# Queries and keys of an encoder layer: keys first in eight stages with open sums in PSUM, queries as ordinary products

## The chip, the cores and the metric

One core of a Trainium2 chip runs the whole program once. The metric is the time of the kernel on the device in microseconds, as the median of several runs. Five engines work side by side and wait for each other by semaphores: TensorE (PE in the profile, with its weight loads as PEld) multiplies matrices into PSUM; VectorE (DVE), ScalarE (ACT) and GpSimd (POOL) do the elementwise work; SyncE (SP) issues the loads and stores.

## What is computed

One layer of a streaming encoder for 512 prompt tokens and 32 sample tokens, model width 1024. Only the start matters here: a conditioning vector `c` gives scale and shift (`w_ada`), the normalized input is modulated to `h`, and `h` is multiplied with `w_in`, whose first 512 columns are the queries of the attention and whose next 512 are its keys.

```python
mod = jnp.einsum('bd,de->be', jax.nn.silu(c), w_ada) + b_ada
sh1, sc1, g1, sh2, sc2, g2 = jnp.split(mod[:, None, :], 6, axis=-1)
h = layer_norm(x) * (1 + sc1) + sh1
z = jnp.einsum('btd,de->bte', h, w_in)
a_q, a_k, a_v, m_qk, m_v, m_if, m_o = jnp.split(z, IN_SPLITS, axis=-1)
a_out = attend(aq, ak, av, lam)                  # differential attention, 4 heads
m_out, m_state = recur(mq, mk, mv, ig, lf)       # mLSTM, 4 heads, chunkwise
y_a = a_n.astype(x.dtype) @ w_br_a
y_b = m_n.astype(x.dtype) @ w_br_b
mix = (g_a * y_a + g_b * y_b) @ w_o
x = layer_norm(ALPHA * x + (1 + g1) * mix, ln1_g, ln1_b)
ffn = (jax.nn.silu(gt) * up) @ w_down            # after the same adaLN scheme, h2 @ w_gu
```

The keys themselves are an output too (`k_rows`), as tokens by features.

## The kernel before

All activations stand as features by tokens: `h` is eight tiles of 128 features by 544 tokens, each in two parts, `hH` and `hL` (a rounded value and what the rounding left), and each weight tile is split likewise into `hi` by ScalarE and `lo` = raw - `hi` by VectorE or POOL. A product of one 128-column tile of weights (an n-tile) with one feature tile takes three matmuls (`hi` with `hH`, `hi` with `hL`, `lo` with `hH`) for each half of the tokens, 256 and 288 columns, the halves named in `HALF`.

At the start, `x_tile` normalizes the four tiles of prompt tokens and transposes them to `xT`, `x_rows` does the sample's rows. `ada_gemv` makes scale and shift of some feature tiles: sixteen small matmuls into a bank `ga`, copied to `gs`; its transposes `gt` are reduced into `modT`, and `modulate` makes `hH` and `hL` from `xT`. The string `ORDER0` sets the order of these steps up to the second half of the first stage.

Queries and keys are made in five stages of 1, 1, 2, 2 and 2 feature tiles (`STAGES`). In each stage `group_split` splits the stage's key columns, then its query columns; for each of the eight n-tiles a `Unit` opens a PSUM bank of the tag `g` (three buffers), runs the stage's matmuls and closes it, and `qk_evac` copies the bank to `qk` (stage 0) or adds it to what the earlier stages left there: by VectorE (`SCALAR_TENSOR_TENSOR` at L176, or ScalarE's `qk_t` and a POOL addition in stage 1). In the last stage each key head is transposed to tokens by features and stored (`k_out`: `k_tok`, `kst`, `k2`).

After that come ordinary products over all eight feature tiles, run by `stream`, which prepares the next unit's weights while one runs: values, gates, the mLSTM's inputs, branch products, output projection and feed-forward. The attention and the mLSTM are a side stream of generators that `Lane` places between the matmuls of the main stream by its own estimates of when each engine is free; so the place of every side instruction in an engine's queue follows from those estimates. The last product of the second branch reads the mLSTM's result `mna`, `mnb`, made from the transposes `onT` for each head of the sample by `gate_split`. All engines' queues run in the order in which they are written.

Weights come by `load` on SP's queue. Raw weights have a ring of two 8 KB buffers (`raw_tile`), and the first stages' weights lie in slots that later tensors take.

Of the kernel before, what the change touches and what calls it, by code (L numbers as in the profile page):

```python
# [33 lines left out]
class Lane:  # L34
    """Emits the steps of generators between the steps of a main stream, by estimates of when each engine gets there."""
# [58 lines left out]
def trunk_kernel(ctx: ExitStack, tc: tile.TileContext, I: dict, O: list):  # L94
# [16 lines left out]
    class Halves:  # L111
        """Eight tiles of features by tokens, held in the two halves of a slot."""
# [103 lines left out]
    ADA_AT = (0, 0)  # L216
    WARM = 0
    STAGES = (1, 1, 2, 2, 2)
    START = tuple(sum(STAGES[:i]) for i in range(len(STAGES)))
    ada_raw, w_raw = {}, {}  # L220

    def load_ada(s, dst):
        w = STAGES[s] * 128
        if not isinstance(dst, list):
            dst = [dst[:, 8 * i * w:8 * (i + 1) * w] for i in range(2)]
        ada_raw[s] = [d[:, 0:8 * w].rearrange("p (k c) -> p k c", k=8) for d in dst]
        for i in range(2):
            c0 = 1024 * i + START[s] * 128
            load(ada_raw[s][i], w_ada[:, c0:c0 + w].rearrange("(k p) c -> p k c", p=128))
# [11 lines left out]
    s2a = [slot(f"2{c}", [128, 2176], F32, f"s2_a{c}") for c in "ab"]  # L241
    s3a = [slot(f"3{c}", [128, 2176], F32, f"s3_a{c}") for c in "ab"]
    s8a = slot(8, [128, 2048], F32, "s8_a")
# [10 lines left out]
    load_ada(0, raw_tile())  # L254
    load_w(0, raw_tile())
# [105 lines left out]
    warm = bank("o", "warm")  # L361

    def keep_warm(n):
        for _ in range(n):
            tr(warm[:, 0:128], ident, 128)
# [50 lines left out]
    def modulate(k, part=None):  # L416
        """Features of tile k: all tokens, or those of one half."""
# [9 lines left out]
        (vtt if part != 0 else gtt)(hL(k)[:, c], t[:, c], hH(k)[:, c].bitcast(F32), SUB)  # L427

    def all_of(gen):
        for _ in gen:  # L430
            pass

    def ada_gemv(s):
        n = STAGES[s]
        w = n * 128
        ga = bank("o" if s % 2 else "x", "ga")
        for i in range(2):
            for k in range(8):
                g = 32 * (k % 4)
                nc.tensor.matmul(  # L440
                    ga[g:g + 32, i * w:(i + 1) * w], scT[:, k, :], ada_raw[s][i][:, k, :], start=(k < 4), stop=(k >= 4)
                )
                lane.pe(0.06 * n)
        return ga

    def ada_first(s, ga=None, part=None):
        n = STAGES[s]
        w = n * 128
        if ga is None:
            ga = ada_gemv(s)  # L450
        yield 0
        gs = tmp([128, 512], "gs")
        vcopy(gs[:, 0:2 * w], ga[:, 0:2 * w])
        yield 0
        gt = bank("x", "gt")
        for b in range(2 * n):
            tr(gt[:, b * 128:(b + 1) * 128], gs[:, b * 128:(b + 1) * 128], 128)
        yield 0
        red = small([128, 4, 2], "red")
        nc.vector.tensor_reduce(  # L460
            out=red[:, 0:2 * n, :], axis=AX.X, op=ADD,
            in_=gt[:, 0:2 * w].rearrange("p (e g c) -> p e c g", g=4, c=32)[:, :, 0:2, :],
        )
        m = modT[:, 0:16, :].rearrange("p (i k) r -> p i k r", i=2)[:, :, START[s]:START[s] + n, :]
        b = PT[:, c_b_ada:c_b_ada + 16].rearrange("p (i k) -> p i k", i=2)[:, :, START[s]:START[s] + n]
        for i in range(2):
            vtt(
                m[:, i], red[:, i * n:(i + 1) * n, :], b[:, i].unsqueeze(2).to_broadcast([128, n, 2]), ADD
            )
        yield 0  # L470
        ms = [modulate(START[s] + k, part) for k in range(n)]
        for g in ms:
            next(g)
        yield 0
        for g in ms:
            all_of(g)

    groups = [(s, i) for s in range(len(STAGES)) for i in range(2)]
    parts = {}

    def group_split(x):
        if x in parts or x >= len(groups):
            return
        s, i = groups[x]
        n = STAGES[s]
        r = w_raw[s][:, i]
        hi = wp.tile([128, 2, 512], F32R, tag="hi", name="hi", bufs=2)
        lo = wp.tile([128, 2, 512], F32R, tag="lo", name="lo", bufs=2)
        act(hi[:, 0:n], r, AF.Copy)
        gtt(lo[:, 0:n], r, hi[:, 0:n].bitcast(F32), SUB)  # L490
        parts[x] = (hi, lo)
# [4 lines left out]
    def first_half():  # L496
        for x in range(2):
            hi, lo = parts[x]
            for h in range(4):
                ps = bank("g", "g")  # L500
                c = slice(128 * h, 128 * h + 128)
                for p, (w, a) in enumerate(((hi, hH), (hi, hL), (lo, hH))):
                    nc.tensor.matmul(ps[:, 0:256], w[:, 0, c], a(0)[:, 0:256], start=(p == 0), stop=(p == 2))
                act(qk_holder["kq"[x]][:, h, 0:256], ps[:, 0:256], AF.Copy, scale=0.125 if x else 1.0)
                yield
# [3 lines left out]
    g0 = None  # L509
    m1 = None  # L510
    fh = first_half()

    def step(c):
        nonlocal g0, m1, ga1
        if c in "0123":
            next(xg[int(c)], None)
        elif c == "r":
            next(xg[4], None)
        elif c == "c":
            next(pc, None)  # L520
        elif c == "g":
            if g0 is None:
                g0 = ada_first(0, ada_gemv(0), 0)
            next(g0, None)
        elif c == "w":
            group_split(len(parts))
        elif c == "h":
            next(fh, None)
        elif c == "m":
            if m1 is None:  # L530
                m1 = modulate(0, 1)
            next(m1, None)
        elif c == "a":
            ga1 = ada_gemv(1)
        elif c == "p":
            load_params(prm_b)

    ga1 = None
    for c in ORDER0:
        step(c)  # L540
    params(prmB, 64)
    load_w(3, raw_tile())
    load_ada(4, slot(6, [128, 4096], F32, "s6_a"))
    load_w(4, raw_tile())
# [26 lines left out]
    class Unit:  # L571
        """One n-tile of a product: its weights' parts, its matmuls, what takes its results."""
# [38 lines left out]
    class IfUnit:  # L611
        """The gates' eight columns: the weights' two parts side by side, so that each half of h passes once."""
# [112 lines left out]
    def to_tok(src, name, tag="x", part=(0, 1)):  # L725
        """[128, T] features by tokens into PSUM as tokens by features: the prompt's four tiles, the sample's."""
# [108 lines left out]
    def qk_evac(s, i, h):  # L835
        def f(ps, hf, o, n):
            dst = qk_holder["kq"[i]][:, h, o:o + n]
            sc = 0.125 if i else 1.0
            if s == 0:
                act(dst, ps[:, 0:n], AF.Copy, scale=sc)  # L840
            elif s == 1 and hf:
                t = tmp([128, 288], "qk_t")
                act(t, ps[:, 0:n], AF.Copy, scale=sc)
                gtt(dst, dst, t, ADD)
            else:
                stt(dst, ps[:, 0:n], sc, dst, MUL, ADD)
                if hf and s == len(STAGES) - 1:
                    if i:
                        q_tasks.append(lane.add(q_split(h)))
                    else:  # L850
                        lane.add(k_out(h), 0.5)
        return f
# [636 lines left out]
    def stage_part(x, j):  # L1489
        def f():  # L1490
            group_split(x)
            if j == 1:
                group_split(x + 1)
            c = slice(j * 128, (j + 1) * 128)
            return tuple(t[:, :, c] for t in parts[x])
# [615 lines left out]
```

## Time and profile before

| | |
|---|---|
| median of 3 runs | 963.54 us (962.74 to 964.62) |
| span of the profiled execution | 966.0 us |
| mean granted TensorE clock in it | 0.982 |
| first key product, first value product | 18.72 us, 98.70 us |
| TensorE, VectorE, ScalarE, POOL busy | 95%, 54%, 37%, 22% |
| moved by DMA | 110.43 MB, 114 GB/s on average |

The profiled execution is one of its own; of it the span from first to last instruction is known, 2.5 us above the median of the runs. In a row of a timeline stand start and duration of an instruction or a run of like ones, then engine, line of the kernel, operation, what it writes and reads, shapes, and in brackets how long the engine was idle before and who ended that. A row of a list of waits gives who waited for whom, the sum in us, how often, and the longest. In a row of stretches stand busy time and count for each engine, the granted clock of TensorE as a share of full speed, the share of the DMA engines and GB/s. A row of groups gives the count, busy time and mean ns of one, then idle time ahead of them. A matmul's duration overlaps with the next one's, so the distance of two starts is what counts.

### The profile page before, as it was taken

Reading aid. Unit: us, or ns where it says so; the run is one execution under the profiler, and the core shown is the slowest. Engines: PE = TensorE matmul, PEld = TensorE weight load, DVE = VectorE, ACT = ScalarE, POOL = GpSimd, SP = SyncE. Lnnn points to the kernel's source line nnn. Section 1 sums busy time; section 2 is a strip of 40 time slices with the busy share of each in tenths; the row PEclk is TensorE's granted clock in tenths of the full one; section 3 lists DMA queues with packets and bytes.
Section 4 is the critical chain, followed back from the end, with each engine's and each line's share of the span. In section 5 each row is a group of like instructions: output and inputs, shape, how many; then the busy total and the mean of one; then the engine's idle time right before and its main releaser. Section 6 shows DMA issues by size and latency. Waiting matters only on the chain. (4 is left out here: it accounts for less than half of the span.)

```text
span 966.0 us, 17335 instructions
## 1 busy us (share of the span) xinstructions
PE 916.9 (95%) x7184; PEld 868.2 (90%) x7184; DVE 525.4 (54%) x1113; ACT 355.8 (37%) x689; POOL 214.1 (22%) x253
## 2 busy tenths in 40 slices
PE   4799999999999999999999989999999999999993
PEld 4679998798798889899999989999999999999993
DVE  4657567877554444446846886544444443223356
ACT  4511466555542332322434474322222222212241
POOL 4433116332411100101741664200000000000014
PEclk8989999999999999999999999999999999999997
DMA  9904423252244244333911502022222226322302
GB/s 281 337 1 127 147 67 112 88 174 89 88 132 143 93 141 133 93 132 124 309 63 45 192 32 89 1 88 88 89 88 88 88 88 232 123 77 77 121 1 92
DMA packets 92283, 110.43 MB, mean 114 GB/s; under 512 B 3897, under 2 KB 75789, under 8 KB 92205
## 3 DMA queue, kind: packets, MB, share of 16 engines
q1 hardware_dynamic: 91996, 109.27, 34.8%
q8 instruction: 56, 0.92, 0.4%
q14 instruction: 23, 0.18, 0.1%
q10 hardware_dynamic: 208, 0.07, 0.0%
HBM read 102.09 MB, written 7.24 MB: 113 GB/s over the span
## 5 line engine op out<-in xcount | busy, mean ns | idle before, releaser
L153 DVE TENSOR_TENSOR lo<-raw,hi 128x1024 fp32r<-128x1024 f32 (+3 forms) x102 | 112.0, 1098 | 130.4 <-ACT hi L132 125.4
L132 ACT ACTIVATE hi<-raw 128x1024 fp32r<-128x1024 f32 (+2 forms) x124 | 122.1, 984 | 153.1 <-PE dn L600 61.6
L600 PE MATMUL dn<-act,hi 128*128 128x288 f32 (+1 forms) x704 | 135.8, 292 | 0.0
L600 PE MATMUL g<-hHa,hi 128*128 128x288 f32 (+1 forms) x344 | 109.1, 317 | 6.2 <-DVE qka L176 4.7
L600 PEld LDWEIGHTS dn<-act,hi 128*128 128x128 f32 x704 | 110.8, 189 | 0.0
L600 PE MATMUL g<-hHb,hi 128*128 128x256 f32 (+1 forms) x352 | 107.8, 306 | 1.3 <-DVE qka L176 1.3
L600 PE MATMUL g<-h2Ha,lo 128*128 128x288 f32 (+1 forms) x352 | 101.4, 288 | 2.4 <-POOL lo L157 1.5
L600 PE MATMUL dn<-act,lo 128*128 128x288 f32 (+1 forms) x352 | 101.8, 289 | 1.8 <-DVE lo L153 1.8
L600 PE MATMUL g<-h2La,hi 128*128 128x288 f32 (+1 forms) x352 | 101.4, 288 | 1.0 <-DVE h2La L153 1.0
L600 PE MATMUL g<-h2Ha,hi 128*128 128x288 f32 (+1 forms) x352 | 102.1, 290 | 0.0
L600 PE MATMUL g<-hLb,hi 128*128 128x256 f32 (+1 forms) x352 | 101.9, 289 | 0.0
L600 PE MATMUL g<-hLa,hi 128*128 128x288 f32 (+1 forms) x344 | 101.2, 294 | 0.8 <-DVE hLa L153 0.7
L600 PE MATMUL g<-h2Hb,hi 128*128 128x288 f32 (+1 forms) x352 | 101.8, 289 | 0.0
L600 PE MATMUL g<-h2Lb,hi 128*128 128x288 f32 (+1 forms) x352 | 101.5, 288 | 0.1
L600 PE MATMUL g<-hHb,lo 128*128 128x256 f32 (+1 forms) x352 | 101.4, 288 | 0.0
L600 PE MATMUL g<-hHa,lo 128*128 128x288 f32 (+1 forms) x344 | 100.7, 293 | 0.2 <-DVE lo L153 0.2
L600 PE MATMUL g<-h2Hb,lo 128*128 128x288 f32 (+1 forms) x352 | 100.8, 286 | 0.0
L157 POOL TENSOR_TENSOR lo<-raw,hi 128x1024 fp32r<-128x1024 f32 (+2 forms) x30 | 63.6, 2122 | 137.1 <-ACT hi L132 126.5
L600 PEld LDWEIGHTS g<-hHa,hi 128*128 128x128 f32 x344 | 66.0, 192 | 23.0 <-issue 6.2
L280 POOL TENSOR_SCALAR rs__10439<-mv__10423 128x1 f32<-128x1 f32 x1 | 0.2, 190 | 322.4 <-DVE mv__10423 L172 322.4
L600 PEld LDWEIGHTS g<-hHb,hi 128*128 128x128 f32 x352 | 66.7, 190 | 5.3 <-issue 2.7
L600 PEld LDWEIGHTS g<-h2Ha,lo 128*128 128x128 f32 x352 | 66.3, 188 | 3.1 <-POOL lo L157 2.0
(490 smaller groups left out, 2180.4 us busy)
## 6 DMA issues: line engine op xcount, KB each, us to landing
raw<-in_w_gu_dram SPq DMA_DIRECT2D x18, 1024.0 KB, 5.1
raw<-in_w_ada_dram SPq DMA_DIRECT2D x16, 1024.0 KB, 5.2
raw<-in_w_in_dram SPq DMA_DIRECT2D x10, 1024.0 KB
raw<-in_w_gate_dram SPq DMA_DIRECT2D x8, 1024.0 KB, 6.7
raw<-in_w_down_dram SPq DMA_DIRECT2D x8, 1024.0 KB, 5.3
wo<-in_w_o_dram SPq DMA_DIRECT2D x4, 1024.0 KB
rawg<-in_w_gu_dram SPq DMA_DIRECT2D x4, 1024.0 KB
raw<-in_w_down_dram SPq DMA_DIRECT2D x3, 768.0 KB
```

The costliest lines, as they stand in the source:

```text
L132: nc.scalar.activation(out=out, in_=in_, func=func, **kw)
L153: nc.vector.tensor_tensor(out=out, in0=in0, in1=in1, op=op)
L157: nc.gpsimd.tensor_tensor(out=out, in0=in0, in1=in1, op=op)
L280: nc.gpsimd.tensor_scalar(out=out, in0=in_, scalar1=scale, scalar2=EPS, op0=MUL, op1=ADD)
L600: nc.tensor.matmul(ps[:, 0:n], w[:, self.k0 + k, :], a(self.ak0 + k)[:, o:o + n], start=(self.first and k == 0 and p == 0), stop=(self.las ...
```

## The change

Keys alone are made in the first part, in eight equal stages of one feature tile. Their sums stay open in PSUM over all stages: six banks (three of `g`, two of `s`, one of `o`), the first halves of two heads sharing one bank. `qk_evac` is gone; the keys are copied once, after the last stage. The modulation (`ada_gemv`, `ada_turn`, `modulate`) runs two stages ahead of the products. The queries follow in four ordinary units over all eight feature tiles, two loads of 1 MB. Weights' `lo` and the first half's `hL` are made by VectorE in this part instead of POOL.

```diff
-    STAGES = (1, 1, 2, 2, 2)
-    ORDER0 = "0p0c1c1wwg0gg21grgr2ghrhhh3hr2r3hr3hrammh"
...
     def load_w(s, dst):
-        n = STAGES[s]
-        w_raw[s] = dst[:, 0:1024 * n].rearrange("p (i k c) -> p i k c", i=2, k=n)
-        for i, c0 in enumerate((512, 0)):
-            r0 = START[s] * 128
-            load(w_raw[s][:, i], w_in[r0:r0 + n * 128, c0:c0 + 512].rearrange("(k p) c -> p k c", p=128))
+        w_raw.append(dst)
+        load(dst, w_in[s * 128:(s + 1) * 128, 512:1024])
...
-    load_ada(1, s8a)
-    load_w(1, s7a[:, 3072:4096])
-    load_ada(2, s2a)
-    load_w(2, s7a[:, 1024:3072])
-    load_ada(3, s3a)
+    for s in range(1, KD):
+        load_stage(s)
...
-        (vtt if part != 0 else gtt)(hL(k)[:, c], t[:, c], hH(k)[:, c].bitcast(F32), SUB)
+        vtt(hL(k)[:, c], t[:, c], hH(k)[:, c].bitcast(F32), SUB)
...
+    def k_split(s):
+        hi = wp.tile([128, 512], F32R, tag="hi", name="hi", bufs=2)
+        lo = wp.tile([128, 512], F32R, tag="lo", name="lo", bufs=2)
+        act(hi, w_raw[s], AF.Copy)
+        vtt(lo, w_raw[s], hi.bitcast(F32), SUB)
+        k_parts0[s] = hi, lo
...
+    def acc_open(hf):
+        if hf == 0:
+            for i in range(2):
+                b = bank("g", "k_acc")
+                for j in range(2):
+                    acc[2 * i + j, 0] = b[:, 256 * j:256 * j + 256]
+        else:
+            for h, tag in enumerate("gsso"):
+                acc[h, 1] = bank(tag, "k_acc")[:, 0:288]
...
+    def k_mm(s, h, hf, passes):
+        hi, lo = k_parts0[s]
+        o, n = HALF[hf]
+        c = slice(128 * h, 128 * h + 128)
+        for p in passes:
+            w, a = ((hi, hH), (lo, hH), (hi, hL))[p]
+            nc.tensor.matmul(
+                acc[h, hf], w[:, c], a(s)[:, o:o + n],
+                start=(s == 0 and p == 0 and (hf == 1 or h % 2 == 0)),
+                stop=(s == KD - 1 and p == 2 and (hf == 1 or h % 2 == 1)),
+            )
...
+    acc_open(0)
+    gs = ada_gemv(1)
+    k_mms(0, (0,), (0, 1, 2))
+    next(xg[3])
...
+    for s in range(1, KD):
+        ahead = s + 2 < KD
+        if ahead:
+            gs = ada_gemv(s + 2)
+        k_mms(s, (0,), (0, 1, 2))
+        if ahead:
+            ada_turn(s + 2, gs)
+            mods[s + 2] = modulate(s + 2)
+            next(mods[s + 2])
+        if s == KD - 1:
+            for h in range(NH):
+                act(qk_holder["k"][:, h, 0:256], acc[h, 0], AF.Copy)
+        k_mms(s, (1,), (0, 1, 2))
+        if ahead:
+            next(mods[s + 2], None)
+            k_split(s + 2)
+    for h in range(NH):
+        act(qk_holder["k"][:, h, 256:T], acc[h, 1], AF.Copy)
...
+    for h in range(NH):
+        lane.add(k_out(h), 1.0 + 2.0 * h)
+    for c in range(2):
+        units += hunits(w_in, c * 256, [q_evac(2 * c), q_evac(2 * c + 1)])
     units.append(Call(lambda: lane.add(setup())))
```

`q_evac` copies a bank to the queries' tensor with the factor 0.125 and, after the second half, starts `q_split`.

On TensorE's queue at the start, from the sample's first statistics product `cmb` on, stands before:

```order
L136 MATMUL cmb<-mv__248,quart 128x2
L503 MATMUL g<-hHa,hi 128x256
L503 MATMUL g<-hLa,hi 128x256
L503 MATMUL g<-hHa,lo 128x256
L503 MATMUL g<-hHa,hi 128x256
```

and now:

```order
L136 MATMUL cmb<-mv__256,quart 128x2
L418 MATMUL ga<-raw,scT 32x128 x16
L471 MATMUL k_acc<-hHa,hi 128x256
L471 MATMUL k_acc<-hHa,lo 128x256
L471 MATMUL k_acc<-hLa,hi 128x256
L471 MATMUL k_acc<-hHa,hi 128x256
```

The second stage's `ga` has moved ahead of the first key product, and the third pass of a product is now the one with `hL`.

Where keys end and queries begin there was no such place before, since both ran in each stage; now ScalarE's queue has there (`qkb` is the keys' tensor, `qka` the queries'):

```order
L132 ACTIVATE hi<-s_a 128x512
L132 ACTIVATE qkb<-k_acc 128x256 x4
L132 ACTIVATE qkb<-k_acc 128x288 x4
L132 ACTIVATE head_row<-ident 32x4
L132 ACTIVATE hi<-raw 128x1024 x2
L132 ACTIVATE qka<-g 128x256
```

and VectorE's:

```order
L147 TENSOR_SCALAR mn_144<-PT 128x4
L153 TENSOR_TENSOR lo<-raw,hi 128x1024 x2
L180 COPY kst<-k_tok_812 128x512
L180 COPY k_820<-k_tok_817 32x128
L180 COPY kst<-k_tok_823 128x512
```

So the first query weights' `hi` stands behind all evacuations of the keys, and the first copy to `kst` behind two `lo`. On TensorE the transposes of the first two heads follow each other after the first three query products.

At the end of the first branch (products with `ana`, `anb`; the second branch reads `mna`, `mnb`) TensorE's queue was before:

```order
L600 MATMUL g<-ana,lo 128x288
L142 MATMUL onT<-ident,on 128x32 x4
L600 MATMUL g<-ana,hi 128x288
L600 MATMUL g<-anb,hi 128x288
L600 MATMUL g<-ana,lo 128x288
L600 MATMUL g<-ana,hi 128x256
```

and 23 more products of that branch followed. Now:

```order
L142 MATMUL onT<-ident,on 128x32 x4
L609 MATMUL g<-ana,hi 128x288
L609 MATMUL g<-anb,hi 128x288
L609 MATMUL g<-ana,lo 128x288
L609 MATMUL g<-mna,hi 128x256
L609 MATMUL g<-mnb,hi 128x256
```

The sample's `onT` has moved 24 products later; only three products stand between it and the second branch.

More of the change, by code (lines that the diff above doesn't have):

```diff
@@ L214, in trunk_kernel @@
     w_in = I["w_in"][0]
-    ADA_AT = (0, 0)
-    WARM = 0
-    STAGES = (1, 1, 2, 2, 2)
-    START = tuple(sum(STAGES[:i]) for i in range(len(STAGES)))
-    ada_raw, w_raw = {}, {}
+    ada_raw, w_raw = [], []
     def load_ada(s, dst):
[L223 to L226, printed above, removed]
+        ada_raw.append([dst[:, 1024 * i:1024 * i + 1024].rearrange("p (k c) -> p k c", k=8) for i in range(2)])
         for i in range(2):
-            c0 = 1024 * i + START[s] * 128
-            load(ada_raw[s][i], w_ada[:, c0:c0 + w].rearrange("(k p) c -> p k c", p=128))
+            c0 = 1024 * i + s * 128
+            load(ada_raw[s][i], w_ada[:, c0:c0 + 128].rearrange("(k p) c -> p k c", p=128))
     def load_w(s, dst):
-        n = STAGES[s]
-        w_raw[s] = dst[:, 0:1024 * n].rearrange("p (i k c) -> p i k c", i=2, k=n)
-        for i, c0 in enumerate((512, 0)):
-            r0 = START[s] * 128
-            load(w_raw[s][:, i], w_in[r0:r0 + n * 128, c0:c0 + 512].rearrange("(k p) c -> p k c", p=128))
+        w_raw.append(dst)
+        load(dst, w_in[s * 128:(s + 1) * 128, 512:1024])
     x_t = slot(6, [128, 4, D], F32, "x_t")
@@ L240, in trunk_kernel @@
     x_s = s7a[:, 0:256]
-    s2a = [slot(f"2{c}", [128, 2176], F32, f"s2_a{c}") for c in "ab"]
-    s3a = [slot(f"3{c}", [128, 2176], F32, f"s3_a{c}") for c in "ab"]
-    s8a = slot(8, [128, 2048], F32, "s8_a")
+    w_k = s7a[:, 256:4352].rearrange("p (s c) -> p s c", s=KD)
     def load_rows(dst, src):
@@ L253, in trunk_kernel, with load_stage @@
     load_x(1)
-    load_ada(0, raw_tile())
-    load_w(0, raw_tile())
+    ada_at = [raw_tile(), raw_tile()] + [slot(i, [128, 2048], F32, f"s{i}_a") for i in (8, "2a", "2b", "3a", "3b", "5a")]
+    def load_stage(s):
+        load_ada(s, ada_at[s])
+        load_w(s, w_k[:, s, :])
+    load_stage(0)
     load_x(2)
@@ L359, in trunk_kernel @@
     xT = Halves(4, F32, "xT")
[L361 to L365, printed above, removed]
     def x_tile(tt):
@@ L426, in modulate @@
         yield 0
-        (vtt if part != 0 else gtt)(hL(k)[:, c], t[:, c], hH(k)[:, c].bitcast(F32), SUB)
-    def all_of(gen):
-        for _ in gen:
-            pass
+        vtt(hL(k)[:, c], t[:, c], hH(k)[:, c].bitcast(F32), SUB)
     def ada_gemv(s):
-        n = STAGES[s]
-        w = n * 128
-        ga = bank("o" if s % 2 else "x", "ga")
+        ga = bank("x", "ga")
         for i in range(2):
@@ L440, in ada_gemv @@
                 nc.tensor.matmul(
-                    ga[g:g + 32, i * w:(i + 1) * w], scT[:, k, :], ada_raw[s][i][:, k, :], start=(k < 4), stop=(k >= 4)
+                    ga[g:g + 32, 128 * i:128 * i + 128], scT[:, k, :], ada_raw[s][i][:, k, :], start=(k < 4), stop=(k >= 4)
                 )
[L443 to L454, printed above, removed]
+                lane.pe(0.06)
@@ L455, in ada_first, with ada_turn @@
+        gs = tmp([128, 256], "gs")
+        vcopy(gs, ga[:, 0:256])
+        return gs
+    def ada_turn(s, gs):
         gt = bank("x", "gt")
-        for b in range(2 * n):
+        for b in range(2):
             tr(gt[:, b * 128:(b + 1) * 128], gs[:, b * 128:(b + 1) * 128], 128)
-        yield 0
-        red = small([128, 4, 2], "red")
+        red = small([128, 2, 2], "red0")
         nc.vector.tensor_reduce(
-            out=red[:, 0:2 * n, :], axis=AX.X, op=ADD,
-            in_=gt[:, 0:2 * w].rearrange("p (e g c) -> p e c g", g=4, c=32)[:, :, 0:2, :],
-        )
@@ L464, in ada_first @@
[L464 to L491, printed above, removed]
+            out=red, axis=AX.X, op=ADD,
@@ new lines, in ada_turn @@
+            in_=gt[:, 0:256].rearrange("p (e g c) -> p e c g", g=4, c=32)[:, :, 0:2, :],
+        )
+        m = modT[:, 0:16, :].rearrange("p (i k) r -> p k i r", i=2)[:, s]
+        b = PT[:, c_b_ada:c_b_ada + 16].rearrange("p (i k) -> p k i", i=2)[:, s]
+        vtt(m, red, b.unsqueeze(2).to_broadcast([128, 2, 2]), ADD)
+    k_parts0 = {}
+    def k_split(s):
[4 more added lines that the diff above has]
+        k_parts0[s] = hi, lo
@@ L493, in trunk_kernel @@
     qk_holder = {}
     qk_holder["q"], qk_holder["k"] = Halves(5, F32, "qk").h
[L496 to L505, printed above, removed]
+    acc = {}
@@ L507, in trunk_kernel, with k_mms @@
+    def k_mms(s, halves, passes):
+        for hf in halves:
+            for h in range(NH):
+                k_mm(s, h, hf, passes)
     xg = [x_tile(tt) for tt in range(4)] + [x_rows()]
     pc = silu_c()
[L509 to L536, printed above, removed]
@@ L538, in trunk_kernel @@
-    ga1 = None
-    for c in ORDER0:
-        step(c)
-    params(prmB, 64)
-    load_w(3, raw_tile())
-    load_ada(4, slot(6, [128, 4096], F32, "s6_a"))
-    load_w(4, raw_tile())
+    for c in "0":
+        next(xg[0])
+    load_params(prm_b)
+    next(xg[0])
+    next(pc)
+    next(xg[1])
+    next(pc, None)
+    k_split(0)
+    next(xg[1])
+    gs = ada_gemv(0)
+    next(xg[0], None)
+    ada_turn(0, gs)
+    first = modulate(0, 0)
+    next(xg[2])
+    next(xg[1], None)
+    next(first)
+    next(xg[4])
@@ new lines, in trunk_kernel @@
+    next(first, None)
+    next(xg[2])
+    next(xg[4], None)
+    acc_open(0)
+    gs = ada_gemv(1)
+    k_mms(0, (0,), (0, 1, 2))
+    next(xg[3])
+    next(xg[4], None)
+    next(xg[2], None)
+    ada_turn(1, gs)
+    next(xg[4], None)
+    next(xg[3])
+    next(xg[4], None)
+    next(xg[3], None)
+    for g in xg:
+        for _ in g:
+            pass
+    k_split(1)
+    params(prmB, 64)
+    second = modulate(0, 1)
+    next(second)
+    mods = {1: modulate(1)}
+    next(second, None)
+    acc_open(1)
@@ new lines, in trunk_kernel @@
+    next(mods[1])
+    gs = ada_gemv(2)
+    k_mms(0, (1,), (0, 1, 2))
+    next(mods[1], None)
+    ada_turn(2, gs)
+    mods[2] = modulate(2)
+    next(mods[2])
+    k_split(2)
+    next(mods[2], None)
+    for s in range(1, KD):
[14 more added lines that the diff above has]
+            k_split(s + 2)
@@ L833, in setup, with q_evac @@
             yield 0
-    def qk_evac(s, i, h):
+    def q_evac(h):
         def f(ps, hf, o, n):
[L837 to L851, printed above, removed]
+            act(qk_holder["q"][:, h, o:o + n], ps[:, 0:n], AF.Copy, scale=0.125)
+            if hf:
+                q_tasks.append(lane.add(q_split(h)))
         return f
@@ L1487, in trunk_kernel @@
     SIDE_AT = 3
[L1489 to L1495, printed above, removed]
-        return f
-    fin = {}
-    def start_ada(s):
-        return lambda: fin.update({s: lane.add(ada_first(s))})
     lane.free = dict.fromkeys(lane.free, lane.t)
     lane.chain = lane.t
-    fin[1] = lane.add(ada_first(1, ga1))
-    def need_h(s):
-        return lambda: lane.until(lambda: fin[s][2])
-    for x, (s, i) in enumerate(groups):
-        for h in range(4):
-            u = Unit(
-                None, 0, STAGES[s], hH, hL, qk_evac(s, i, h), ak0=START[s], split=stage_part(x, h),
-                halves=(0, 1) if s else (1,),
-            )
-            if i + h == 0 and s:
-                u.need = need_h(s)
-            units.append(u)
-            if (i, h) == ADA_AT and 0 < s and s + 1 < len(STAGES):
-                units.append(Call(start_ada(s + 1)))
+    for h in range(NH):
+        lane.add(k_out(h), 1.0 + 2.0 * h)
+    for c in range(2):
+        units += hunits(w_in, c * 256, [q_evac(2 * c), q_evac(2 * c + 1)])
     units.append(Call(lambda: lane.add(setup())))
@@ L1533, in trunk_kernel @@
     units += vq
-    vch = [u.chunk for u in units if u.chunk]
-    vch[0].gate = lambda: 7 in parts
-    vch[-1].gate = lambda: 9 in parts
     units.append(IfUnit())
```

1 line of the change is left out of this document (added).

## The prediction

> **What bounds the kernel now.** I read the page first, then the list of waits over the first 95 us, the busy time in short stretches, and the timelines of TensorE, VectorE and ScalarE up to the first value product and around 455 us.
>
> ```profile
> span 966.0 us, 17335 instructions
> PE 916.9 (95%) x7184; PEld 868.2 (90%) x7184; DVE 525.4 (54%) x1113; ACT 355.8 (37%) x689; POOL 214.1 (22%) x253
> ...
> PE g L600 <- DVE qka L176: 6.0, 3, 3.5
> ...
> PE g L600 <- ACT qka L132: 1.5, 1, 1.5
> ```
>
> TensorE is busy 95% of the span. Whatever moves the end has to take idle time or half-clock time away from it, or add some. In the query and key stages it waits 6.0 us in three pieces for VectorE's additions into `qka` and once 1.5 us on ScalarE. The clock column tells what a wait costs beyond itself:
>
> ```profile
> core 0: us, PE busy (x) PEld busy (x) DVE busy (x) ACT busy (x) POOL busy (x), PEclk, DMA share, GB/s
> 0.00:15.50 15.50, 4.76 (x47) 3.89 (x47) 4.64 (x12) 5.02 (x8) 7.04 (x20) 1.00 0.86 253
> 0.00:20.00 20.00, 7.10 (x56) 5.61 (x57) 8.59 (x25) 7.70 (x12) 9.25 (x24) 0.93 0.92 266
> 32.00:34.00 2.00, 0.59 (x2) 0.39 (x3) 1.02 (x2) 1.67 (x5) 0.26 (x1) 1.00 1.09 349
> 34.00:36.00 2.00, 2.00 (x11) 2.00 (x11) 0.69 (x2) 0.82 (x2) 1.51 (x2) 0.53 1.08 366
> 44.00:46.00 2.00, 0.00 (x0) 0.00 (x0) 2.00 (x5) 0.59 (x1) 1.34 (x2) 1.00 1.03 369
> 48.00:50.00 2.00, 1.32 (x5) 0.89 (x5) 1.78 (x2) 1.29 (x2) 2.00 (x2) 0.50 0.01 3
> 64.00:66.00 2.00, 0.75 (x6) 0.54 (x5) 2.00 (x5) 0.00 (x0) 0.00 (x0) 1.00 0.00 0
> 66.00:68.00 2.00, 2.00 (x18) 2.00 (x17) 1.07 (x3) 0.00 (x0) 0.00 (x0) 1.00 0.00 0
> ```
>
> After the idle 1.4 us of 32 to 34 the granted clock is 0.53, after the idle at 44 it is 0.50 a little later, and after the 1.25 us of 64 to 66 it stays 1.00. So a gap of about 1.5 us or more in a few microseconds is followed by half clock, a shorter one is not.
>
> ```profile
> 20.12 0.41 PE L503 MATMUL g<-hHa,hi 128*128 128x256 f32 x1
> 22.47 0.41 PE L503 MATMUL g<-hHa,lo 128*128 128x256 f32 x1
> 24.69 1.04 PE L142 MATMUL ps_x<-ident,x_t 128*128 128x128 f32 x8
> 26.23 1.08 PE L440 MATMUL ga<-s_a,scT 128*32 128x128 f32 x32
> 27.25 0.39 PE L503 MATMUL g<-hHa,hi 128*128 128x256 f32 x1
> 89.12 0.71 PE L142 MATMUL k_tok<-ident,qkb 128*128 128x128 f32 x5
> 89.59 0.38 PE L600 MATMUL g<-hHb,hi 128*128 128x288 f32 x1
> 98.70 0.28 PE L600 MATMUL g<-hHa,hi 128*128 128x256 f32 x1
> 100.58 0.28 PE L600 MATMUL g<-hHb,hi 128*128 128x256 f32 x1
> 102.00 0.29 PE L600 MATMUL g<-hHa,hi 128*128 128x288 f32 x1
> 103.60 0.29 PE L600 MATMUL g<-hHb,hi 128*128 128x288 f32 x1
> ```
>
> Here start to start counts. At full clock twelve matmuls of 256 columns take 1.42 us (100.58 to 102.00), twelve of 288 take 1.60; eleven of 256 at half clock take 2.35. A modulation product of one stage (`ga`) takes 1.02, a key's transposes 0.47. The value products begin at 98.70: that is the mark. Up to there both kernels do the same TensorE work; what follows is nearly the same order.
>
> **The change, part by part.** *Start.* The second `ga` now stands ahead of the first key product, so stage 0 waits for the second stage's modulation weights, which lie 4.6 MB deep in the loads (2.1 MB of inputs, 0.1 of the sample, 2.1 of two `w_ada` stages, 0.26 of keys).
>
> ```profile
> 15.50 1.29 DVE L168 BATCH_NORM_STATS2 st__220<-x_t 128x6 f32<-128x512 f32 x2 [3.09 <-DMA x_t<-in_x_prompt_dram]
> ...
> 23.23 0.81 DVE L149 TENSOR_SCALAR x_t<-x_t,mv__284,rs__286 128x1024 f32<-128x1024 f32 x1
> 24.75 0.41 DVE L149 TENSOR_SCALAR s_a<-s_a,rows_c,rs__308 128x256 f32<-128x256 f32 x1 [0.72 <-POOL rs__308 L157]
> 25.76 0.69 DVE L180 COPY xTb<-ps_x 128x512 f32<-128x512 f32 x1 [0.60 <-PE ps_x L142]
> 26.37 0.64 DVE L149 TENSOR_SCALAR mod_t<-xTa,modT 128x256 f32<-128x256 f32 x2
> 27.52 0.46 DVE L153 TENSOR_TENSOR hLa<-mod_t,hHa 128x288 fp32r<-128x288 f32 x1 [0.51 <-ACT hHa L132]
> 28.59 0.41 DVE L180 COPY gs<-ga 128x256 f32<-128x256 f32 x1
> ...
> 11.86 0.63 ACT L132 ACTIVATE hi<-raw 128x512 fp32r<-128x512 f32 x1 [3.02 <-DMA raw<-in_w_in_dram]
> 28.70 1.60 ACT L132 ACTIVATE qkb<-g 128x288 f32<-128x288 f32 x4 [0.33 <-PE g L600]
> ```
>
> Before, the third input tile (byte 3.15 MB) is usable at 15.50, when 15.5 x 253 = 3.9 MB have moved: 0.75 MB of lag. 4.6 + 0.75 = 5.35 MB is reached at 20.0 (20 x 266). So the second `ga` ends at about 21.0; before, key products were running at 20.12. The twelve first-half products then take 2.56 at half clock (21.0 to 23.6), the third tile's transposes 1.04 to 1.5, the `gt` pair 0.3: 25.3. From there one chain runs through VectorE: reduction and bias 0.5 (estimate), fourth tile's normalization 0.81, transposes 1.04, copy 0.69, sample rows 0.41, their transposes and two copies 0.95 (estimate from the shares above), `hi` 0.63, `lo` 0.69, `PT` and `mod_t` 0.9, `hHa` and `hLa` 0.9: with small hops 33.0. The twelve second-half products end at 34.4 (full clock) or 35.5 (half). TensorE idles about 4 us between 25 and 33, so I take half clock for one spell: the loop of stages 1 to 7 starts, in full-clock time, at 36.4 (34.7 if the clock holds).
>
> *Loop.* Per stage 1.42 + 1.60 of keys, 1.02 `ga`, 0.22 `gt` and about 0.3 for the switches: 4.56, five times; the last two stages have no `ga`, 3.05 each. Sum 29.0: 65.4. I cost the modulation and the splits at nothing. VectorE has to do `gs` 0.41, `mod_t` and `hL` about 1.3, `lo` 0.69 and 0.4 of small ones, 2.8 us in 4.5, and each result is asked for a stage later. If that cover went, each us late would show in each stage. All waits on `qka` are gone with the additions (7.5 us with ScalarE's one), and half clock behind two of them. POOL loses its splits of the weights and its additions, none of which TensorE waited for by name, and stands still; the split of `hL` for the first half goes from it to VectorE (0.46, in the 21 us before `ga` ends). SP issues two loads of 512 KB and one of 256 KB a stage, ahead of the two query loads, which wait for the first two `ga` (21 us) and not for anything late; the first value load behind them waits for the second query `lo`, near 70, and is needed near 97.
>
> *From keys to queries.* The last four key evacuations stand on ScalarE ahead of the first query weights' `hi`, and `lo` behind it on VectorE:
>
> ```profile
> L132 ACT ACTIVATE hi<-raw 128x1024 fp32r<-128x1024 f32 x100 | 105.6, 1056 | 105.2 <-PE g L600 36.8 <-PE dn L600 31.2 <-issue 24.2
> L153 DVE TENSOR_TENSOR lo<-raw,hi 128x1024 fp32r<-128x1024 f32 x72 | 88.2, 1224 | 95.0 <-ACT hi L132 91.1 <-PE qk_ps L136 3.7
> ```
>
> TensorE stops for the last evacuation 0.4, hops and a small copy 0.35, `hi` 1.06, `lo` 1.22, less two products that need no `lo`: 2.8. After three products two heads' key transposes follow each other; the second pair needs the buffer of the first, whose copy to `kst` (0.69, as `xTb`) stands on VectorE behind the second unit's `lo` (1.22): another 1.2. Together 4.0, which I count with one spell of half clock, 1.7 (an estimate: 3.4 us at half, the whole row of 34 to 36 and some of the next). Bounds of that clock term: 0, and 3.4, twice the spell. The query weights themselves were loaded long before: 12.7 MB of stages and 2.1 MB of queries at about 350 GB/s are in by 47.
>
> *Queries.* Four units of 24 x (0.118 + 0.133) = 6.04: 24.2, and four key transposes 1.9. So 65.4 + 4.0 + 1.7 + 24.2 + 1.9 = 97.2, against 98.7: 1.5 us earlier.
>
> *The side stream.* The hand-over to the last branch product moves closer:
>
> ```profile
> 454.69 0.28 PE L600 MATMUL g<-mna,hi 128*128 128x256 f32 x1
> 456.10 0.30 PE L600 MATMUL g<-mna,hi 128*128 128x288 f32 x1
> ...
> 451.26 0.19 DVE L176 SCALAR_TENSOR_TENSOR gg<-og,onT 128x32 f32<-128x32 f32 x1 [0.73 <-PE onT L142]
> 451.84 0.25 DVE L176 SCALAR_TENSOR_TENSOR mnb<-gg,mn,mna 128x32 fp32r<-128x32 f32 x1 [0.39 <-ACT mna L132]
> 456.65 0.25 DVE L176 SCALAR_TENSOR_TENSOR mnb<-gg,mn,mna 128x32 fp32r<-128x32 f32 x1 [0.39 <-ACT mna L132]
> ```
>
> Before, the transposes `onT` are used at 451.26, 3.4 us ahead of the branch product of 454.69, and the last head's `mnb` (456.65) is in time for its second-half product, the fourth at 0.4 each from 456.10. Now only three products stand between `onT` and that branch. Four heads at 0.83 each (451.26 to 452.09), with an evacuation and a `lo` between them, end 4.9 us after `onT` starts; the second half asks for head 0 after 2.3 and for the others each 0.4 later: a loss of 1.2. In attention the places of the side work move by a few products in both directions; I put nothing, with 2 us either way, a third of the 6 us that TensorE waits there now (estimate).
>
> **Sum.** -1.5 + 1.2 = -0.3 us. The profiled span is 966.0, 2.5 above the median of the runs; the difference is carried over to the median: 963.54 - 0.3 = 963.2.
>
> **Rivals.** *Faster: the clock holds over both gaps.* Then the loop starts at 34.7 and the transition costs 4.0 alone: 1.7 + 1.7 less, 959.8. For it: the idle time in 25 to 33 and behind the keys is broken up by short work. Against it: the row of 34 to 36, half clock behind 1.4 us idle. The Trainium skill, TensorE: Matmul & The Clock Gate, What's actually happening, says that the clock falls to half after at least one whole idle window of about 3.4 us. By that rule neither gap would be paid and this rival would hold; the trace disagrees, since 1.4 us were enough at 32 to 34.
>
> *Slower: the second modulation weights come late.* They are now in TensorE's queue ahead of all key products, and each load of these weights brings 128 columns (512 B) of a row at a time. If they land at 24 instead of 20, everything behind moves by 4: 967.2. It decides from 22.3 on (1.9 us slower). Against it: 15.50 and 20.00 above, which had such runs in them. The same size comes from half clock lasting two spells at both gaps.
>
> **How the numbers follow.** 0.2% of 963.5 is 1.9 us, about what the runs can tell. My forecast, within that: 0.38. Faster (clock holds, or the branch hand-over costs nothing together with a better attention order): 0.33. Slower: 0.29, of it late weights 0.15, longer half clock 0.14. The range runs from the faster rival less 1.3 of attention to the slower one with as much: 958.5 to 968.5; the likeliest case alone spans 961.6 to 965.4.
>
> **What would show it.** In the changed trace: second `ga` ends near 21; stage 1 begins near 35 to 36; no waits of TensorE between stages 1 and 7; about 4 us of waits on `lo` and `kst` at 65 to 71, with clock 0.5 behind them; first value product near 97; about 1.2 us of waits on `mna` and `mnb` at the last branch. It is wrong if the value products start before 95 or after 99.5, or if attention moves by over 2 us.

## The result and the profile after

The changed kernel takes 978.2 us (976.96 to 979.48, 4 runs), the kernel before 963.14 (962.39 to 964.62, 4 runs): a ratio of 1.0157, 95% interval 1.0139 to 1.0175. It is 15 us slower, where 963.2 had been predicted. The page of the profile after begins so:

```profile
span 975.2 us, 17448 instructions
PE 919.6 (94%) x7280; PEld 870.7 (89%) x7280; DVE 502.8 (52%) x1074; ACT 353.1 (36%) x683; POOL 188.0 (19%) x234
```

A run's time is 1.7 to 1.8 us above its span, so the trace after (975.2) shows the fastest of the four runs, while the trace before (966.0, a time near 967.8) shows a slower one than any of the four. So the two traces show only 9.2 of the 15 us. TensorE's timeline of the changed kernel at the marks of the prediction:

```profile
19.81 1.08 PE L418 MATMUL ga<-raw,scT 128*32 128x128 f32 x16 [0.26 <-DMA raw<-in_w_ada_dram]
20.82 0.58 PE L471 MATMUL k_acc<-hHa,hi 128*128 128x256 f32 x1
34.41 0.39 PE L471 MATMUL k_acc<-hHa,hi 128*128 128x256 f32 x1
63.32 0.29 PE L471 MATMUL k_acc<-hLb,hi 128*128 128x288 f32 x1
65.14 0.39 PE L609 MATMUL g<-hHa,hi 128*128 128x256 f32 x1 [1.53 <-ACT hi L132]
66.40 0.39 PE L609 MATMUL g<-hHa,lo 128*128 128x256 f32 x1 [0.76 <-DVE lo L153]
68.23 1.33 PE L142 MATMUL k_tok<-ident,qkb 128*128 128x128 f32 x5 [0.57 <-DVE kst L180]
94.64 0.28 PE L609 MATMUL g<-hHa,hi 128*128 128x256 f32 x1
462.63 0.28 PE L609 MATMUL g<-mna,hi 128*128 128x256 f32 x1
```

The value products begin at 94.64, 4.06 us ahead of before (98.70). The first product of the last branch begins at 462.63, 7.94 behind before (454.69). So 12.0 us are lost in the 368 us between, where the main products are the same in both kernels and only the side stream (attention, mLSTM) stands at other places. Summed over stretches of 2 us in this part, TensorE is idle for 13.9 us after and 6.3 before, and loses 5.1 us after and 1.7 before to a granted clock below 1 (busy time multiplied by what is missing to 1): together 11.1 of the 12.0. From there to the end another 1.3 go. TensorE's waits between 95 and 500 us, after:

```profile
PE o_ps L136 <- ACT wT L132: 4.0, 1, 4.0
PE gt L142 <- ACT wT L132: 3.1, 1, 3.1
PE onT L142 <- DVE on L153: 1.6, 1, 1.6
```

and the two longest of the same list of before, which has no row of that kind above 2 us:

```profile
PE s_ps L1111 <- DVE mx L992: 1.6, 2, 1.5
PE g L600 <- DVE mixLb L153: 1.3, 1, 1.3
```

The two long waits are single stops, near 143 and near 219. Stretches around them, after:

```profile
144.00:148.00 4.00, 0.63 (x3) 0.67 0.01 2
148.00:152.00 4.00, 4.00 (x22) 0.50 0.01 4
220.00:224.00 4.00, 2.13 (x9) 0.56 0.01 4
224.00:228.00 4.00, 4.00 (x22) 0.59 0.00 0
```

(TensorE's busy time and count, the granted clock, then the DMA.) Behind each stop the clock is at half for some 5 us of work, which costs about 2.5 us more (an estimate from these rows). Two stops with their half clock come to 4.0 + 2.5 + 3.1 + 2.5 = 12 us. Before has no such stop, but one spell of half clock in this part, so the comparison is that of the sums above: 7.7 us more of idle time, 7.1 of it the two stops, and 3.4 more lost to the clock; 0.9 stays unassigned. What the stops wait for is seen on ScalarE, whose wT the rows name. The timeline of after, with POOL's and SP's rows for the load:

```profile
134.42 2.55 POOL L157 TENSOR_TENSOR lo<-raw,hi 128x1024 fp32r<-128x1024 f32 x1 [15.67 <-ACT hi L132]
137.00 0.38 SPq L184 DMA_DIRECT2D raw<-in_w_in_dram  x1
143.06 1.06 ACT L132 ACTIVATE hi<-raw 128x1024 fp32r<-128x1024 f32 x1 [2.63 <-DMA raw<-in_w_in_dram]
144.13 1.28 ACT L132 ACT_TABLE_LOAD   x1
145.43 0.72 ACT L132 ACTIVATE s_m<-s_m,mx 128x512 f32<-128x512 f32 x1
...
146.85 0.47 ACT L132 ACTIVATE wT<-wT_ps 128x384 f32<-128x384 f32 x1
...
220.49 1.06 ACT L132 ACTIVATE hi<-raw 128x1024 fp32r<-128x1024 f32 x1 [6.05 <-DMA raw<-in_w_in_dram]
221.45 0.36 ACT L132 ACTIVATE wT<-wT_ps 128x256 f32<-128x256 f32 x1
```

The wT copy itself is short. Ahead of it in ScalarE's queue stands the split `hi` of the next unit's weights, and that waits for its load. The load was issued at 137.00, when POOL had done the `lo` that freed its buffer, and took 6.1 us. TensorE stops at 143.4, when the load has just landed; what it then waits for is the split, a table load of 1.28 us, two exponentials and the copy, which ScalarE could have begun in the 2.6 us in which it waited for the load. The exponentials of `s_m` had their inputs since 138.8 (VectorE's `mx`) and stood behind the split all the same; the Trainium skill, PSUM — Partial Sum Buffer, Engine vs sequencer instructions, says that ScalarE's queue is strictly first in, first out, and the trace agrees: they start at 145.43. In the kernel before the same load takes as long (issued at 138.19, split at 144.54), and ScalarE waits for it too (0.5 us), but the wT copy that the attention needs next stands ahead of the split. SP's and ScalarE's timeline of before:

```profile
138.19 0.39 SPq L184 DMA_DIRECT2D raw<-in_w_in_dram  x1
...
140.68 0.36 ACT L132 ACTIVATE wT<-wT_ps 128x256 f32<-128x256 f32 x1
...
144.54 1.06 ACT L132 ACTIVATE hi<-raw 128x1024 fp32r<-128x1024 f32 x1 [0.54 <-DMA raw<-in_w_in_dram]
```

The lists of ScalarE's waits from 95 to 260 us have nearly the same sum for such loads in both kernels, 8.5 us before and 9.0 after (the sum, how often, the longest):

```profile
ACT hi L132 <- DMA raw<-in_w_in_dram: 8.5, 4, 4.2
```

```profile
ACT hi L132 <- DMA raw<-in_w_in_dram: 9.0, 3, 6.0
```

The theory taken to the chip: the estimates of `Lane` know no loads. A change in the first part shifts where they place one early step of the side stream, all later steps follow, and two splits that wait for loads come to stand ahead of attention steps that TensorE needs. The rival: keys and queries leave the loads, buffers or the clock in a worse state.

### The profile page after: what moved, and what is told of

It reads as the page before. It is cut to its first block, busy times and chain, and to the rows that moved or that the text cites. A ratio compares the mean times of both kernels' runs of the same rounds, so it can differ in the third digit from the quotient of the medians.

```text
span 975.2 us, 17448 instructions
## 1 busy us (share of the span) xinstructions
PE 919.6 (94%) x7280; PEld 870.7 (89%) x7280; DVE 502.8 (52%) x1074; ACT 353.1 (36%) x683; POOL 188.0 (19%) x234
## 4 chain that ended last, share of the span: by engine, by line
PE 82%; DVE 8%; DMA 3%; ACT 3%; SPq 2%; issue 1%; POOL 1%; ACTq 0%; POOLq 0%; DVEq 0%
PE g L609 56%; PE dn L609 13%; PE k_acc L471 2%; SPq L184 2%; PE ga L306 1%; DVE lo L153 1%; DMA raw<-in_w_in_dram 1%; PE o_ps L136 1%; PE mo_ps L136 1%; PE qk_ps L136 1%; ACT hi L132 1%; PE s_ps L1108 1%; PE res_ps L142 1%; POOL lo L157 1%; DMA prmB<-in_b_gate_dram 1%
## 5 line engine op out<-in xcount | busy, mean ns | idle before, releaser
L609 PE MATMUL g<-hHa,hi 128*128 128x256 f32 (+1 forms) x320 | 101.9, 318 | 1.5 <-ACT hi L132 1.5
L609 PE MATMUL g<-hHb,hi 128*128 128x256 f32 (+1 forms) x320 | 97.4, 304 | 0.0
L609 PE MATMUL g<-hHa,lo 128*128 128x256 f32 (+1 forms) x320 | 92.6, 289 | 1.5 <-DVE lo L153 0.8
L609 PE MATMUL g<-hLa,hi 128*128 128x256 f32 (+1 forms) x320 | 92.8, 290 | 0.0
L609 PE MATMUL g<-hLb,hi 128*128 128x256 f32 (+1 forms) x320 | 92.8, 290 | 0.0
L609 PE MATMUL g<-hHb,lo 128*128 128x256 f32 (+1 forms) x320 | 92.5, 289 | 0.0
L609 PEld LDWEIGHTS g<-hHa,hi 128*128 128x128 f32 x320 | 61.0, 191 | 17.5 <-issue 7.1
L157 POOL TENSOR_TENSOR lo<-raw,hi 128x1024 fp32r<-128x1024 f32 (+1 forms) x24 | 53.1, 2212 | 116.5 <-ACT hi L132 107.4
L609 PEld LDWEIGHTS dn<-act,lo 128*128 128x128 f32 x352 | 66.9, 190 | 2.3 <-DVE lo L153 2.2
L609 PEld LDWEIGHTS g<-h2La,hi 128*128 128x128 f32 x352 | 66.1, 188 | 1.2 <-DVE h2La L153 1.2
```

The source lines that it names most:

```text
L157: nc.gpsimd.tensor_tensor(out=out, in0=in0, in1=in1, op=op)
L609: nc.tensor.matmul(ps[:, 0:n], w[:, self.k0 + k, :], a(self.ak0 + k)[:, o:o + n], start=(self.first and k == 0 and p == 0), stop=(self.las ...
```

## The experiments

Ratios are to the kernel before on the same chip, where its median was 963.2 to 965.0 us. The edits are shown abridged; `...` marks a gap.

**e1, e2: the order exchanged.** The places of all side steps from the first value products on are written out as a table (calls of the lane, name of the task) and taken from the other kernel; every engine's queue from there on is then that of the other kernel.

```diff
     def run(self):
+        if self.plan is not None:
+            return self._follow()
...
     def start_side():
+        lane.follow(PLAN)
         state["side"] = lane.add(side_all())
```

> The changed kernel, with the order of the side stream (attention and mLSTM among the main products) from the first value products on written out as it is in the kernel before; keys and queries stay as changed. Theory (the keys and queries gain about 4.1 us, value products at 94.64 instead of 98.70, and the whole loss comes from another order of the same side work): 963.1 - 4.1 = 959, between 957 and 961.5. Rival (the new first part leaves loads, weight buffers or the clock in a worse state for what follows, whatever the order): still 972 to 978. Half and half would lie at 965 to 970.

Measured: 962.53 us (959.56 to 964.01), ratio 0.998 (0.9964 to 0.9997). The rival falls: with the order of before, the changed keys and queries are even a little faster than before. The gain is 2.5 us, not 4.1, and the time lies above the 957 to 961.5 that were expected. The 4.1 came from one pair of traces: in the trace of e1 the value products begin at 97.41, only 0.8 to 1.3 us ahead of the two traces of before (98.70, and 98.16 in e3).

> The kernel before, with the side stream from the first value products on in the order that the changed kernel has; keys and queries as before. Theory: all of the loss moves over, 963.1 + 12.0 (attention, from the traces) + 1.2 (hand-over) = 976 by the traces and up to 982 by the runs. Rival (the state left by the first part): 962 to 966.

Measured: 978.87 us, ratio 1.0149 (1.0123 to 1.0175), with both stops in TensorE's list of waits:

```profile
PE o_ps L228 <- ACT wT L224: 4.3, 1, 4.3
PE gt L234 <- ACT wT L224: 2.9, 1, 2.9
```

The order alone carries 13.8 us into a kernel that has none of the other changes. From the first value product to the first of the last branch, the traces give 356.0 (before), 355.8 (e3, below) and 354.1 us (e1) in the order of before, and 368.0 (after) and 366.9 (e2) in that of the changed kernel.

The program written out, without a run, shows how near the two orders lie: nearly the same queues as in e1 come out, from the first steps of the side stream on, if the changed kernel starts the preparing task `setup` 2 us later in the estimates (0.5 us changes no queue, 4 us gives yet another order). In the changed kernel that task is one step further when the side stream starts: nine steps done instead of eight.

**e3: before once more.**

> The kernel before with its own order written out as a table instead of found by the estimates: the same program, for a second trace. Time 963.1 within 1. The first trace of before had a span of 966.0, some 4 us more than its runs; theory: this span is 961 to 963, and the half clock around 156 to 162 us of the first trace is not there or is shorter. Rival: half clock there again and a span near 966, so that the trace itself costs something.

Measured: 965.07 us, ratio 0.9997 (0.998 to 1.0013), span 965.3. My theory falls here: the half clock is there again, at the same place.

```profile
156.00:158.00 2.00, 2.00 (x12) 0.67 0.85 298
158.00:160.00 2.00, 2.00 (x11) 0.50 0.00 0
```

The half clock and the span near 966 are what the rival had expected, but its reason, a cost of the trace, isn't needed: the 23 runs of before on that chip lie between 959.72 and 967.12, and this execution, at 966.97, inside that range.

**e4: loads made known to the estimates.**

```diff
     def emit(self):
+        self.at = max(lane.chain, lane.t) + 6.0
...
     def prepare(self):
         lane.begin()
+        if self.chunk is not None:
+            lane.chain = max(lane.chain, self.chunk.at)
```

> The changed kernel; the estimates by which side steps are placed now hold that a unit's weights arrive 6 us after their buffer came free, so that ScalarE's split of them counts as late and side steps are put behind it only if they can wait. Theory (the loss is TensorE waiting for attention steps that stand on ScalarE behind a split which waits for its load: 4.0 us near 143 and 3.1 near 220, with half clock behind each): most of it goes, 962 to 969. Rival (the loss is spread over many small shifts or comes from VectorE): 973 to 980.

Measured: 975.34 us, ratio 1.0128 (1.0093 to 1.0162). In this order the kernel's outputs are no longer the layer's (why was not followed), so it counts as the time of an order and not as a version. Both stops are gone from the list, and branch a begins at 423.52, as early as in e1 (423.25). But side work that was held back comes due at the end: from there to branch b it takes 36.1 us, in e1 28.3, with waits like this one for the sample's mLSTM:

```profile
459.16 0.50 PE L142 MATMUL onT<-ident,on 32*128 32x32 f32 x2 [2.78 <-DVE on L149]
```

The expected time, 962 to 969, was missed, and by the time the rival's range holds: the two stops go, and 7.8 us more than in e1 are lost between the branches.

**e5: two splits moved.** The changed kernel's own order, but the two splits of 143.06 and 220.49 are written some steps into the unit that runs, not ahead of it (each `hi` on ScalarE, with its `lo` on POOL). `HOLD` names the two units and the number of steps.

```diff
+HOLD = {(12, 8): 9, (24, 8): 3}
...
+            if (i, u.nk if isinstance(u, Unit) else 0) in HOLD:
+                lane.later = (lane.calls + HOLD[i, 8], split_next)
-            if isinstance(u, Unit):
+            elif isinstance(u, Unit):
                 prep(i + 1)
```

> The changed kernel with its own order everywhere, but for two instructions on ScalarE: the weight splits (hi, and their lo) that waited for their loads at 143.06 and 220.49 us are written later in the queue, behind the attention's exponentials and wT copies that stood behind them. Theory (these two waits, each with half clock behind it, are most of the loss): both stops of TensorE go, 4.0 + 3.1 us, and some 2.5 us of half clock behind each: 978 - 12 = 966, between 963 and 970. Rival (the stops are only moved: the units whose splits come later now wait instead, or other side steps do): 973 to 979.

Measured: 969.27 us (967.39 to 971.64), ratio 1.005 (1.0032 to 1.0067), from 1.0157: about 10 us less, by two splits. The splits now stand at 148.13 and 224.04. The one stop is gone, the other down to 0.3, and the first row here is the longest wait that is left between the value products and the last branch:

```profile
PE wT_ps L241 <- DVE s_att L275: 2.1, 1, 2.1
...
PE o_ps L235 <- ACT wT L231: 0.3, 1, 0.3
```

**e9, e10: the loads made earlier.** The order stays as it is; a load of two n-tiles comes in two halves, the columns of the first one first (in the edit, words stand for the expressions).

```diff
     def hunits(W, col0, evacs, eng=None):
-        ch = wchunk(W, 0, 8, col0)
+        if W is w_in and col0 >= 512:
+            views = [(half j of the buffer, columns col0 + 128 * j on) for j in range(2)]
+            ch = Chunk(views)
+        else:
+            ch = wchunk(W, 0, 8, col0)
```

> The changed kernel, its own order on every engine; only the loads of w_in behind the queries come in two halves each, the 128 columns of the first n-tile ahead of those of the second. Theory (a split waits for its load and the attention waits behind the split): half a load lands some 1.5 us sooner, so TensorE's stops of 4.0 near 143 and 3.1 near 220 become 2.5 and 1.6, and half clock may stay away from the second: 3 to 6 us less than 978, that is 972 to 975 (a ratio of 1.008 to 1.012 beside 964.9). Rival (lateness of loads plays no part, only the order): 977 to 979, a ratio of 1.014 to 1.016.

Measured: 971.7 us (969.39 to 974.6), ratio 1.0082 (1.006 to 1.0103). No instruction changes its place on TensorE, VectorE, ScalarE or POOL, and some 7 us go. The second split now starts 4.3 us after its load's issue (213.76 to 218.04), where the undivided load took 5.6 (214.88 to 220.49). The first split waits only 0.5 us for its load now, and yet 1.9 us of that stop are left: the split, the table load and the exponentials still stand ahead of the wT copy. So not only the lateness of the load but the split's place itself costs time. The stops are shorter, and the clock stays up behind the second:

```profile
PE o_ps L228 <- ACT wT L224: 1.9, 1, 1.9
PE gt L234 <- ACT wT L224: 1.8, 1, 1.8
```

```profile
140.00:150.00 10.00, 8.12 (x53) 0.83 0.36 99
...
214.00:224.00 10.00, 7.61 (x57) 1.00 0.42 107
224.00:234.00 10.00, 10.00 (x82) 1.00 0.45 142
```

> The sixth run's kernel (order of the kernel before, first query split early) with the same halved loads. Theory: in this order little waits behind the late splits (ScalarE waits 4.7 us for loads, TensorE not behind it), so at most 1 us is gained: 957 to 958.5, a ratio of 0.992 to 0.993. Rival (late loads cost time in this order too): 954 to 956.

Measured: 958.08 us, ratio 0.9938 (0.9919 to 0.9958), no different from e6 below (0.9928, on another chip). ScalarE's wait for loads from 95 to 260 falls from 5.0 us in e6 to 1.5, and no gain is seen, to within the 2.5 us or so that the intervals leave open. In an order in which TensorE does not wait behind a late split, an earlier load gained nothing that could be measured.

**e7, e8: other orders.** The changed kernel with the one edit `lane.add(setup(), 4.0)`, and with 6.0.

> The changed kernel; the side stream's preparing task (distances, gate weights) is started 4 us later in the estimates, nothing else is edited; this gives a third order of the attention's steps up to about 230 us, and the changed kernel's own order behind that. Theory (the order of these steps decides): a time of its own, away from 978 by 3 us or more, most likely between 964 and 975. Rival (only the keys and queries and what they leave behind count): 976 to 980.

Measured: 978.45 us, ratio 1.0138 (1.0118 to 1.0158): the same time as the changed kernel, against my expectation. By the time alone the rival would stand. The trace, of the slowest of its four runs (981.8), shows the same mechanism at another place: a stop of 5.7 us of `v_tok` for `anb`, which waits for `ana`, which stands on ScalarE behind a split waiting for its load.

```profile
PE v_tok L142 <- DVE anb L176: 5.7, 1, 5.7
```

```profile
223.07 1.06 ACT L132 ACTIVATE hi<-raw 128x1024 fp32r<-128x1024 f32 x1 [4.88 <-DMA raw<-in_w_in_dram]
224.03 0.67 ACT L132 ACTIVATE ana<-onT,da 128x512 fp32r<-128x512 f32 x1
```

> As the run before with 6 us instead of 4: a fourth order, different up to the last branch product. Theory: again a time of its own, between 960 and 978. Rival: 976 to 980.

Measured: 972.13 us, ratio 1.008 (1.0055 to 1.0105). In this order the output for the sample's tokens is no longer the layer's; it counts as the time of an order. It has no stop above 1 us behind a split that waits for its load. Orders of the same work thus gave 962.5, 972.1, 978.2 and 978.5 us with the same keys and queries.

**e6: the gap between keys and queries closed**, on top of e1 (in the edit, words stand for some expressions).

```diff
         if s == KD - 1:
+            q_raw = raw_tile()
+            load(q_raw, columns 0 to 255 of w_in)
+            act(q_hi, q_raw's first n-tile, AF.Copy)
+            vtt(q_lo, q_raw's first n-tile, q_hi, SUB)
             for h in range(NH):
                 act(qk_holder["k"][:, h, 0:256], acc[h, 0], AF.Copy)
...
-        lane.add(k_out(h), 1.0 + 2.0 * h)
+        lane.add(k_out(h), 2.0 + 4.0 * h)
```

> The first run's kernel (changed keys and queries, side stream in the order of the kernel before), and the first query unit's weights are split ahead of the last key evacuations instead of behind them; the keys' transposes start 2, 6, 10 and 14 us into the queries instead of 1, 3, 5 and 7. Theory (TensorE's waits of 1.5 and 0.8 at the first query and 0.6 to 1.4 on kst, with half clock behind, are lost time): 3 to 4 us less than the first run, about 959 beside 965 for the kernel before on that chip, a ratio of 0.993 to 0.995. Rival (the last evacuations, now later, stop TensorE just as long, or the clock falls anyway): 962 to 963, a ratio of 0.998.

Measured: 958.37 us (955.73 to 958.83), ratio 0.9928 (0.9911 to 0.9945). TensorE has no wait from 50 to 95 us and no half clock from 40 to 95. Its value products begin at 92.38, in e1 at 97.41. By the ratios it gains 5 us on e1, a little more than the 3 to 4 expected. This version beats both kernels, by 6.5 us the one before; two edits are in it, and what each is worth was not separated.

## Why the prediction was wrong, point by point

- *Start.* Second `ga` to end at 21.0: 20.8. The sum of the loop begins with stage 1's `ga`; that was to start at 36.4, or 34.7 if the clock holds. It starts at 33.40 in the profiled execution, where the granted clock shows 1.00 in all stretches from 18 to 42 (but see the last section for the first products), and at 36.30, 35.72 and 35.64 in e1, e5 and e7, which have the same instructions there and half clock in much of 18 to 36. Both cases occur, from one execution to the next. The chain through VectorE is shorter than forecast: the second-half products start at 31.16, not at 33.0, so that 36.4 for the slower case is right in part by luck.
- *Loop.* 29.0 us: 30.0 (33.40 to the last product's start at 63.32 and its end near 63.4), and 29.9 in e1, e5 and e7. The prediction expected no wait in it; in the profiled execution there is one of 1.7 for `gs` at 37.76, so to cost the modulation at nothing did not hold there; it is more than the 1.0 by which the forecast is short.
- *From keys to queries.* 4.0 of waits and 1.7 of half clock, 5.7 in all: from 63.4 to the values 31.2, less 24.2 and 1.9, leaves 5.1. The waits that the list names were 1.53, 0.76 and 0.57, 2.9 together; in e5 and e7, with half clock from 68 to 76, 6.5 to 6.8 are left by the same sum.
- *First value product.* 97.2: 94.64 here, below the 95 that was named as a sign of being wrong; 97.41, 98.49, 98.19 and 95.92 in e1, e5, e7 and e9. The forecast lies amid these; "faster, the clock holds" (3.4 us less, 93.8) was nearest to this one. Before varies as well: 98.70, 98.16, and 95.45 in e2.
- *Hand-over to the last branch.* +1.2: +1.3, by the mechanism that was forecast. The twelve second-half products of the branch's first unit take 2.70 us (464.06 to 466.76), before 1.59, with gaps ahead of the second, third and fourth head.
- *Attention, the step that failed.* "I put nothing, with 2 us either way, a third of the 6 us that TensorE waits there now": it cost 12.0 in the traces, and 13.8 as an order alone (e2). Of the 2 us either way, the range took in 1.3. I sized a reordering by the waits that the old order has. That order's waits say how well it avoids the late loads, not how late they are. What showed instead is TensorE waiting for wT copies that stand on ScalarE behind splits that wait for their loads: stops of 4.0 and 3.1 us and half clock behind each. The scale of it stood in another list, ScalarE's 8.5 us of waiting for loads of weights (4.2 the longest), which the prediction does not use, because TensorE did not wait behind it. With these 8.5 and two spells of half clock at 2.5 the slow side would have reached 963.2 + 13.5 = 976.7 (an estimate after the fact, and still 1.5 short of the time measured).
- *Rivals.* The second `ga` waited 0.3 us for its weights here; in e1 the two first `ga` waited 1.1 and 0.6, and the second ended at 21.3. Weights 4 us late, as the rival had it, did not occur. None of the rivals was an order in which TensorE waits behind a late split.

The sum of the parts is not exact: e1 (-2.5) and e2 (+13.8) make +11.3, the changed kernel showed +15.1; by their intervals, 8.4 to 16.6 and 13.4 to 16.9. Of the order's cost, e5 accounts for some 10 us; the rest I did not separate (waits of 1 to 2 us, `onT` 1.6 and the hand-over among them, are candidates). Which rule of the estimates moves everything when `setup` is one step further was not followed step by step either.

## What to carry to other kernels

Where a planner without knowledge of loads sets the order of queues, any edit ahead of it is also a new order of everything behind it: write the old order out and keep it while the edit is measured, or the two effects can't be told apart. For the scale of what a new order can cost, add up what each engine waits for in the old one, hidden or not, since a hidden wait can become a stop for whatever comes to stand behind it. The sum is no bound: here it was 8.5 us on ScalarE, and the order cost 13.8, since half clock came on top and a stop of 4.0 grew from a wait of 2.6. An instruction that waits for a load goes behind the work whose inputs are there; done for two splits, that brought some 10 us.

## What was not expected of the hardware

- The clock fell to half after waits of 1.53 and 0.76 us (at 65 to 66; granted 0.86 and 0.72 in 64 to 68 and 68 to 72), and not after 1.8 us in e9 (1.00 from 214 to 234). In before, waits of 1.51 (at 33.3) and 1.47 (at 155.8) were followed by 0.50; in after, waits of 1.67 (at 37.8) and 1.57 (at 279.9) were followed by 1.00. So the reading in the prediction, that a gap of about 1.5 us or more is followed by half clock, doesn't hold, and the length of a wait alone doesn't tell it. The Trainium skill, TensorE: Matmul & The Clock Gate, What's actually happening, asks for at least one idle window of about 3.4 us; the waits named here that were followed by half clock, all shorter, disagree with that, e9 doesn't.
- The clock column can miss a spell: the products from 21.20 on start 0.21 us apart, as at half clock, in a stretch that shows 1.00. TensorE's timeline of after, and the stretch:

```profile
21.20 0.42 PE L471 MATMUL k_acc<-hHa,lo 128*128 128x256 f32 x1
21.41 0.41 PE L471 MATMUL k_acc<-hLa,hi 128*128 128x256 f32 x1
```

```profile
18.00:22.00 4.00, 3.74 (x39) 1.00 1.14 304
```

- The same program varied by 7 us between runs on one chip (959.72 to 967.12), with granted clocks from 0.983 to 0.990; a single trace of it can lie 4 us off its median (966.0, a time near 967.8, beside 963.14).
